# Products of zeros on TensorE ahead of the first transposes

## The chip, the cores and the metric

The kernel runs on one core of a Trainium2 chip. Its engines each work through their own list of instructions: TensorE (PE; its weight loads are shown as PEld), VectorE (DVE), ScalarE (ACT), GpSimd (POOL), and SyncE (SP), which here only issues transfers. They wait for each other by semaphores. The metric is the device time of one execution in microseconds, as the median of several.

## What is computed

One step of a streaming encoder layer for a prompt of 1024 tokens and a sample of 32, both 1024 wide. Cut to what stands at the start, which is where the change is:

```python
mod = silu(c) @ w_ada + b_ada                       # c: one row for the prompt, one for the sample
sh1, sc1, gt1, sh2, sc2, gt2 = split(mod, 6)        # six parts, each 1024 wide
h = rmsnorm(x, g_mix) * (1 + sc1) + sh1             # rmsnorm: x * rsqrt(mean(x * x) + EPS) * g
u = h @ w_in                                        # 1024 -> 5640 columns
# then band attention (8 heads), an mLSTM (4 heads), two gated branches, an output
# projection, a residual add, and the same pattern again with a SwiGLU feed-forward
```

All is float32. Large products are made from a high and a low part of each factor in a reduced float32 format (`F32R`), in three passes: high by high, low by high, high by low.

## The kernel before

**Tiling.** Prompt and sample form one matrix of 1056 columns (tokens), kept transposed: 8 blocks of 128 features on the partitions, tokens along the rows of memory. Products take the tokens in three tiles of 352 columns. [...]

**The start.** The order of work on TensorE, ScalarE, VectorE and GpSimd is the order in which the code writes it (a manual schedule); each engine runs its list strictly in that order. SyncE's transfers are issued in code order too.

- L222 to L229 issue the loads of the input, 8 blocks of 128 tokens (`xtok`, 512 KB each), and of the sample (`xsm`). Parameters go to `prow` from GpSimd's queue.
- `load_ada` (L276) issues 8 loads of `w_ada` of 1 MB each, one block of 128 rows each: the columns of the shift and the scale.
- The loop at L299 goes over four groups of two input blocks. For each it makes square sums on VectorE (`square_sum`, L288) and 16 transposes on TensorE (`x_transposes`, L296), four to one PSUM bank; ScalarE copies each bank to memory (L297). Three such banks (`mm`) are in turn.
- Between the third and the fourth group's transposes `param_cols` stands: TensorE transposes the parameters (L239), VectorE copies them (L240), ScalarE makes `csil`, the SiLU of `c` (L241). That copy stands between square sums 5 and 6 in VectorE's list.
- After the loop the sample is transposed (L310) and copied (L312), and GpSimd turns the square sums into the reciprocal roots `rstd` (L313, L314).
- `first_ada` (L331) walks over the 8 blocks of `w_ada`. In each step TensorE multiplies the scale's columns by `csil` (L337) into the PSUM tile `psA`, and VectorE adds the shift's columns times `csil` into two sums `acv` (L327 for the first block, L329 for the others). After the first step TensorE spreads `rstd` over the partitions (L257).
- `row_sums` (L363, L367), `first_shift` (L375) and `first_scale` (L380, L381) finish shift and scale. Then `first_units` (L482) makes the normed input block by block on VectorE and ScalarE (L390 to L409), and TensorE starts the products with `w_in` (L490). The weights' high and low parts for it come from `first_split` (L476) and `first_low` (L480) into tiles of the pool `wsp`, which has four buffers of 128x1024.
- SyncE also writes the transposed input to `xres` in device memory (L1540), once L312 is done.

**After the start.** All later products run through `unit` (L458) and similar loops (L906, L1843, L2089, L2246). Weight blocks are loaded ahead (L434) and split into parts on ScalarE (L424) and VectorE or GpSimd (L425).

Of the kernel before, what the change touches and what calls it, by code (L numbers as in the profile page):

```python
# [9 lines left out]
F32R = mybir.dt.float32r  # L10
BF16 = mybir.dt.bfloat16
# [6 lines left out]
P = 128  # L18
# [121 lines left out]
def hybrid_stream_step(  # L140
# [11 lines left out]
    pe, act, dve, pool, sp = nc.tensor, nc.scalar, nc.vector, nc.gpsimd, nc.sync  # L152
# [9 lines left out]
    wsp = ctx.enter_context(tc.tile_pool(name="wsp", bufs=4))  # L162
# [11 lines left out]
    def nm(s):  # L174
        uid[0] += 1
        return f"{s}_{uid[0]}"

    def slot(shape, dt=F32):
        return slots.tile(shape, dt, tag="s", name=nm("s"))

    def tmpt(shape=(P, T), dt=F32):
        return tmp.tile(list(shape), dt, tag="t", name=nm("t"))

    def mmt():
        return mm.tile([P, 512], F32, tag="mm", name=nm("mm"))
# [4 lines left out]
    def ps_t():  # L190
        return ps.tile([P, 1024], F32, tag="PT", name=nm("psT"))
# [4 lines left out]
    def f(ap):  # L196
        return ap.bitcast(F32)
# [12 lines left out]
    pool.memset(ssq, 1.0)  # L210


    prow = tmpt((P, P))
    xtok = []

# [60 lines left out]
    def load_ada(n):  # L276
        while len(was) < n:
            wa = slot([P, 2048])
            sp.dma_start(wa, w_ada[len(was) * P:(len(was) + 1) * P, 0:2048])
            was.append(wa)  # L280

    load_ada(KD)

    def square_sum(i):
        n = P if i < 8 else TS
        src = xtok[i] if i < 8 else xsm
        junk = tmpt((P, D), BF16)
        dve.tensor_tensor_reduce(junk[:n], src, src, 1.0, 0.0, ALU.mult, ALU.add, ssq[:n, i:i + 1])  # L288
# [18 lines left out]
    for j0 in range(0, KD, 4):  # L307
        pt = mmt()
# [142 lines left out]
    def unit(w, w0, xt, lo, hi, last=True):  # L451

        wt = W.use(w)
        pt = mmt()
        n = len(xt)
        for k in range(n):
            for q, (a, b) in enumerate(PASSES):
                pe.matmul(pt[:, :hi - lo], wt[(w0 + k) // 4][:, a, (w0 + k) % 4], xt[k][:, b, lo:hi],  # L458
                          start=(k == 0 and q == 0), stop=(k == n - 1 and q == 2))
            if k % 2 == 0 and k:  # L460
                side.flush(1)
            if k % 2 == 1:
                side.tick()
        if last:
            W.used(w)
        return pt[:, :hi - lo]
# [1308 lines left out]
    for pi, tiles in enumerate(parts):  # L1775
        if pi == 1:
            job = side.start(second_norm(parts[0]), 15, 50)
        for j in range(KD):
            for lo, hi in tiles:
                pt = unit(w_o[pi][j], 0, merged, lo, hi)  # L1780
# [50 lines left out]
    def bank(n=NT):  # L1831
        i = turn[0] % 8
        t = pb.tile([P, 512], F32, tag=f"b{i}", name=nm("psb")) if i < 5 else mmt()
        turn[0] += 1
        return t[:, :n]

    def times(w, x, acc, start=True, stop=True, onto=False):


        wt, = W.use(w)  # L1840
        for k in range(4):
            for q, (a, b) in enumerate(PASSES):
                pe.matmul(acc, wt[:, a, k], x[k][:, b], start=(start and not onto and k == 0 and q == 0),  # L1843
                          stop=(stop and k == 3 and q == 2), skip_group_check=onto)
        W.used(w)
        return acc
# [11 lines left out]
    def fifteen_products(x, rows, done, beside):  # L1858


        first = set()
        left = [(i, n) for ps in PARTS.values() for i, n, _ in ps]
        banks = {}
        for w, r in zip(x.blocks, x.FORMS):
            beside(r)
            if r in ONTO:
                y = times(w, FORMS[r], banks.pop(ONTO[r]), onto=True)
            else:
                y = times(w, FORMS[r], bank())
                banks[r] = y  # L1870
            complete = []
            for i, n, sign in PARTS[r]:
                c = rows[i][:, thirds[n]]
                if (i, n) not in first:
                    first.add((i, n))
                    if r == 8 and i == 1:
                        dve.tensor_copy(c, y)
                    else:
                        act.activation(c, y, AF.Copy, scale=float(sign))
                else:  # L1880
                    dve.tensor_tensor(c, c, y, op=ALU.add if sign > 0 else ALU.subtract)
                left.remove((i, n))
                if (i, n) not in left:
                    complete.append((i, n))
            run_put_off()
            put_off.extend(lambda z=z: done(*z) for z in complete)
# [34 lines left out]
    for i in range(0, len(fifteen), 2):  # L1921
# [5 lines left out]
        def run(x, rows):  # L1927
            fifteen_products(x, [y for _, _, y in rows], lambda i, n: rows[i][0].complete(*rows[i][1:], n), late_steps)
# [119 lines left out]
    for c in range(2):  # L2048
# [14 lines left out]
        x = times(a1, FORMS[14], bank())  # L2063
# [18 lines left out]
    for j in range(KD):  # L2082
        wt = W.use(w_d0[j])
        n = 0
        for i in range(2):
            acc = bank()
            for k in range(KP):
                for q, (u, v) in enumerate(PASSES):
                    pe.matmul(acc, wt[k // 4][:, u, k % 4], piece_of[k, i][:, v],  # L2089
                              start=(k == 0 and q == 0), stop=(k == KP - 1 and q == 2))  # L2090
# [144 lines left out]
    for j in range(KD):  # L2235
# [4 lines left out]
        for w, (k0, k1) in zip(w_d1[j], chunks):  # L2240
            wt = W.use(w)
            for k in range(k0, k1):
                while steps and (min(k + 4, NF - 1), 2) not in piece_of:
                    steps.pop(0)[2]()
                for q, (u, v) in enumerate(PASSES):
                    pe.matmul(acc, wt[(k - k0) // 4][:, u, (k - k0) % 4], piece_of[k, 2][:, v],  # L2246
                              start=(k == 0 and q == 0), stop=(k == NF - 1 and q == 2))
# [47 lines left out]
```

## Time and profile before

| what | value |
|---|---|
| time, median of 3 runs | 1606.86 us (1606.58 to 1607.44) |
| span of the profiled execution, first to last instruction | 1604.4 us |
| TensorE busy | 1576.2 us, 98% of the span |
| VectorE, ScalarE, GpSimd busy | 1135.5, 786.2, 445.3 us |
| TensorE's granted clock, mean | 0.999 |
| DMA, mean over the span | 120 GB/s |
| DMA, first two fortieths of the span | 362 and 273 GB/s |

The profile is of one execution. The median is 2.46 us longer than the profiled span; the time of the profiled execution itself is not recorded beside its span. "Busy" of TensorE is the union of the spans of its products, which overlap since they are pipelined, so that a row's mean duration (322 ns for a product of 352 columns) is longer than the distance from one product to the next.

A row of the timeline gives the start in microseconds from the span's start, the length, the engine, the line, the operation, what it writes and reads, the number of instructions merged into the row, and in brackets how long the engine was idle before it and what ended that.

### The profile page before, as it was taken

Reading aid. Unit: us, or ns where it says so; the run is one execution under the profiler, and the core shown is the slowest. Engines: PE = TensorE matmul, PEld = TensorE weight load, DVE = VectorE, ACT = ScalarE, POOL = GpSimd, SP = SyncE. Lnnn points to the kernel's source line nnn. Section 1 sums busy time; section 2 is a strip of 40 time slices with the busy share of each in tenths; the row PEclk is TensorE's granted clock in tenths of the full one; section 3 lists DMA queues with packets and bytes.
Section 4 is the critical chain, followed back from the end, with each engine's and each line's share of the span. In section 5 each row is a group of like instructions: output and inputs, shape, how many; then the busy total and the mean of one; then the engine's idle time right before and its main releaser. Section 6 shows DMA issues by size and latency. Waiting matters only on the chain.

```text
span 1604.4 us, 27406 instructions
## 1 busy us (share of the span) xinstructions
PE 1576.2 (98%) x10256; PEld 1554.8 (97%) x10256; DVE 1135.5 (71%) x2185; ACT 786.2 (49%) x1747; POOL 445.3 (28%) x477
## 2 busy tenths in 40 slices
PE   7999999999999999999999999999999999999997
PEld 6989999999999999999999999999999999999997
DVE  7766564646776855556654699988888986799754
ACT  3665463544455644444443655554544444545443
POOL 2344243433332411000012100566565650000001
PEclk9999999999999999999999999999999999999999
DMA  9823323232222232675353311313222227427453
GB/s 362 273 77 91 97 82 102 88 122 86 67 80 80 69 95 69 121 276 168 121 153 113 106 54 48 100 55 105 81 79 94 67 82 252 135 79 250 135 156 126
DMA packets 210414, 192.45 MB, mean 120 GB/s; under 512 B 10706, under 2 KB 180618, under 8 KB 209258
## 3 DMA queue, kind: packets, MB, share of 16 engines
q1 hardware_dynamic: 205386, 187.82, 37.4%
q10 hardware_dynamic: 4640, 2.82, 0.6%
q8 instruction: 81, 1.33, 0.4%
q14 instruction: 51, 0.42, 0.1%
q0 software_dynamic: 256, 0.06, 0.0%
HBM read 152.19 MB, written 41.63 MB: 121 GB/s over the span
## 4 chain that ended last, share of the span: by engine, by line
PE 88%; DVE 5%; DMA 3%; ACT 2%; issue 1%; SPq 0%; ACTq 0%; POOL 0%; DVEq 0%; POOLq 0%
PE mm L458 39%; PE psb L1843 18%; PE mm L1843 10%; PE mm L2246 3%; PE mm L906 3%; PE psb L2246 2%; PE psV L805 2%; PE psb L2089 2%; PE psS L747 1%; DMA s<-in_w_ada_dram 1%; PE psT L774 1%; PE mm L2089 1%; DMA wraw<-in_w_in_dram 1%; DMA t<-in_x_sample_dram 1%; DVE s L390 1%
## 5 line engine op out<-in xcount | busy, mean ns | idle before, releaser
L458 PE MATMUL mm<-s,wsp 128*128 128x352 f32 x4104 | 689.1, 324 | 0.0
L458 PEld LDWEIGHTS mm<-s,wsp 128*128 128x128 f32 x4104 | 656.9, 188 | 2.0 <-issue 0.4
L425 DVE TENSOR_TENSOR wsp<-wraw,wsp 128x512 fp32r<-128x512 f32 (+1 forms) x280 | 234.9, 855 | 120.0 <-ACT wsp L424 118.0
L1843 PE MATMUL psb<-s,wsp 128*128 128x352 f32 x1611 | 271.7, 322 | 1.5 <-DVE wsp L425 0.8
L424 ACT ACTIVATE wsp<-wraw 128x512 fp32r<-128x512 f32 x336 | 199.5, 617 | 141.5 <-PE psb L1843 44.0
L1843 PEld LDWEIGHTS psb<-s,wsp 128*128 128x128 f32 x1611 | 260.6, 188 | 2.1 <-DVE wsp L425 1.1
L1843 PE MATMUL mm<-s,wsp 128*128 128x352 f32 x933 | 159.3, 322 | 0.0
L1843 PEld LDWEIGHTS mm<-s,wsp 128*128 128x128 f32 x933 | 151.2, 188 | 0.5 <-DVE wsp L425 0.5
L767 POOL TENSOR_SCALAR st<-st,mx 128x640 f32<-128x640 f32 (+5 forms) x72 | 55.7, 774 | 184.8 <-DVE mx L766 170.5
L1229 DVE SCALAR_TENSOR_TENSOR t<-wa,cmix,t 128x512 f32<-128x512 f32 x112 | 89.1, 801 | 15.0 <-DMA wa<-in_w_ada_dram 14.6
L425 POOL TENSOR_TENSOR wsp<-wraw,wsp 128x512 fp32r<-128x512 f32 x56 | 75.8, 1374 | 49.4 <-ACT wsp L424 47.9
L762 ACT ACTIVATE st<-st,mx 128x640 f32<-128x640 f32 (+5 forms) x72 | 47.9, 666 | 71.6 <-DVE mx L761 70.3
L761 DVE CUSTOM_DVE_ANT_0 st<-psS,bias 128x640 f32<-128x640 f32 (+5 forms) x72 | 44.3, 616 | 46.1 <-PE psS L747 33.2
L1790 POOL TENSOR_TENSOR t<-t,sl 128x352 f32<-128x352 f32 x19 | 18.3, 961 | 185.3 <-DMA wraw<-in_w_out_dram 130.8
L781 ACT ACTIVATE pT<-psT 128x640 fp32r<-128x640 f32 (+3 forms) x80 | 38.6, 493 | 63.1 <-PE psT L774 47.7
L2158 POOL TENSOR_TENSOR fst<-fst 128x1 f32<-128x1 f32 (+1 forms) x6 | 1.2, 192 | 236.6 <-ACT t L2151 236.6
L786 DVE TENSOR_TENSOR pT<-psT,pT 128x640 fp32r<-128x640 f32 (+3 forms) x80 | 43.9, 557 | 22.5 <-ACT pT L781 22.3
L1452 POOL TENSOR_TENSOR wraw<-wraw,raw 128x512 f32<-128x512 f32 x33 | 55.8, 1702 | 0.9
L906 PE MATMUL mm<-s,s 128*128 128x264 f32 (+3 forms) x432 | 54.8, 283 | 0.0
L2246 PE MATMUL mm<-s,wsp 128*128 128x352 f32 x330 | 54.4, 324 | 0.0
L2246 PEld LDWEIGHTS mm<-s,wsp 128*128 128x128 f32 x330 | 53.1, 188 | 0.0
L1452 POOL TENSOR_TENSOR spare<-wraw 128x512 f32<-128x512 f32 x11 | 16.5, 1496 | 130.0 <-DMA wraw<-in_w_gate_up_dram 122.4
(396 smaller groups left out, 2561.3 us busy)
## 6 DMA issues: line engine op xcount, KB each, us to landing
wraw<-in_w_in_dram SPq DMA_DIRECT2D x38, 512.0 KB, 4.0
wraw<-in_w_gate_up_dram SPq DMA_DIRECT2D x33, 512.0 KB, 3.8
wa<-in_w_ada_dram SPq DMA_DIRECT2D x64, 256.0 KB, 2.9
wraw<-in_w_down_dram SPq DMA_DIRECT2D x32, 512.0 KB, 4.0
a_d<-t SPq DMA_DIRECT2D x22, 528.0 KB, 2.8
g_d<-t SPq DMA_DIRECT2D x16, 528.0 KB, 3.9
x<-xres SPq DMA_DIRECT2D x16, 528.0 KB, 6.7
t<-g_d SPq DMA_DIRECT2D x16, 528.0 KB, 5.4
```

The source lines that it names most:

```text
L424: act.activation(dst[:, 0], src, AF.Copy)
L425: eng.tensor_tensor(dst[:, 1], src, f(dst[:, 0]), op=ALU.subtract)
L458: pe.matmul(pt[:, :hi - lo], wt[(w0 + k) // 4][:, a, (w0 + k) % 4], xt[k][:, b, lo:hi], start=(k == 0 and q == 0), stop=(k == n - 1 and q ...
L761: dve.tensor_tensor_reduce(so, sv, bi, -1.0, 3.0e38, ALU.add, ALU.min, mx[:n, 1:2])
L762: act.activation(st[:n, :w], st[:n, :w], AF.Exp, bias=mx[:n, 1:2], scale=-1.0, accum_out=mx[:n, 2:3])
L767: pool.tensor_scalar(st[:n, :w], st[:n, :w], mx[:n, 3:4], 1.0, op0=ALU.mult, op1=ALU.mult)
L906: pe.matmul(pt[:n, :wd], hs[k][:, a, i * P:i * P + n], whl[b][:, k, :wd], start=(k == 0 and q == 0), stop=(k == KD - 1 and q == 2))
L1229: dve.scalar_tensor_tensor(ac[:, c], wa, cmix[:, c, k:k + 1], ac[:, c], op0=ALU.mult, op1=ALU.add)
L1452: self.eng.tensor_tensor(a(dst), a(x), a(y), op=op)
L1843: pe.matmul(acc, wt[:, a, k], x[k][:, b], start=(start and not onto and k == 0 and q == 0), stop=(stop and k == 3 and q == 2), skip_group_ ...
L2089: pe.matmul(acc, wt[k // 4][:, u, k % 4], piece_of[k, i][:, v], start=(k == 0 and q == 0), stop=(k == KP - 1 and q == 2))
L2246: pe.matmul(acc, wt[(k - k0) // 4][:, u, (k - k0) % 4], piece_of[k, 2][:, v], start=(k == 0 and q == 0), stop=(k == NF - 1 and q == 2))
```

## The change

A function `warm_up` is called after the loads of `w_ada` are issued and ahead of the loop over the four groups.

```diff
+    def warm_up():
+
+        z = wsp.tile([P, 1024], F32R, tag="wsp", name=nm("wsp"))
+        zb = z.bitcast(BF16)
+        dve.memset(f(z), 0.0)
+        pt = ps_t()
+
+        def run(x, w, n):
+            pe.matmul(pt[:, :n], w, x, start=True, stop=True)
+
+        for _ in range(12):
+            run(z[:, 0:352], z[:, 512:640], 352)
+        for o in (0, 8, 4, 16, 2):
+            for _ in range(5):
+                run(z[:, o:o + 352], z[:, 512:640], 352)
+        for o in (0, 8):
+            for _ in range(4):
+                run(z[:, o:o + 512], z[:, 520:648], 512)
+        for n in (352, 512):
+            for _ in range(5):
+                run(zb[:, 0:n], zb[:, 1024:1152], n)
...
     load_ada(KD)
+    warm_up()
```

VectorE fills one 128x1024 tile of the weight pool with zeros. TensorE then multiplies parts of that tile with each other: 37 products of 352 columns in `F32R`, 25 of them from shifted starts, 8 of 512 columns in `F32R`, and 5 each of 352 and 512 columns with the same bytes read as bfloat16. All write to one PSUM tile, which `first_ada` later takes for `psA`; nothing reads what they write. The lines behind the two places move down, by 22 and 23: L296 becomes L319, L239 becomes L261, L337 becomes L360.

TensorE's list from its beginning, before (`ident` is the identity, `s_92` and `s_95` hold input blocks, `mm` are PSUM banks):

```order
L2291 UNCONDITIONAL_BRANCH
L296 MATMUL mm_143<-ident,s_92 128x128 x4
L296 MATMUL mm_149<-ident,s_92 128x128 x4
L296 MATMUL mm_155<-ident,s_92 128x128 x4
L296 MATMUL mm_161<-ident,s_92 128x128 x4
L296 MATMUL mm_171<-ident,s_95 128x128 x4
```

The same list now, to the first transpose (`wsp_139` is the tile of zeros, `psT_141` the PSUM tile):

```order
L2314 UNCONDITIONAL_BRANCH
L221 MATMUL psT_141<-wsp_139 128x352 x37
L221 MATMUL psT_141<-wsp_139 128x512 x8
L221 LDWEIGHTS wsp_139
L221 MATMUL psT_141<-wsp_139 128x352
...
L221 LDWEIGHTS wsp_139
L221 MATMUL psT_141<-wsp_139 128x512
L319 MATMUL mm_201<-ident,s_92 128x128 x4
```

The 55 products stand ahead of all transposes; those of bfloat16 have a weight load of their own in the list. From the first transpose on the list is as before, with other line numbers.

VectorE's list from its beginning, before (ISA stands for the square sum and the reading of its result, `t` is scratch):

```order
L2291 UNCONDITIONAL_BRANCH
L288 ISA t_139,ssq<-s_92 128x1024
L288 ISA ssq 128x1
L288 ISA t_141,ssq<-s_92 128x1024
L288 ISA ssq 128x1
```

And now:

```order
L2314 UNCONDITIONAL_BRANCH
L217 MEMSET wsp_139 128x1024
L311 ISA t_197,ssq<-s_92 128x1024
L311 ISA ssq 128x1
L311 ISA t_199,ssq<-s_92 128x1024
```

One row came in front, and the rest is unmoved. The first product on TensorE waits for that memset. The lists of ScalarE, GpSimd and SyncE hold the same rows in the same order as before.

## The prediction

> **What bounds the kernel now.** I read the page first, for which engine sets the end.
>
> ```profile
> span 1604.4 us, 27406 instructions
> ...
> PE 1576.2 (98%) x10256; PEld 1554.8 (97%) x10256; DVE 1135.5 (71%) x2185; ACT 786.2 (49%) x1747; POOL 445.3 (28%) x477
> ...
> PE 88%; DVE 5%; DMA 3%; ACT 2%; issue 1%; SPq 0%; ACTq 0%; POOL 0%; DVEq 0%; POOLq 0%
> ```
>
> TensorE is busy for 98% of the span and carries 88% of the chain that ended last. The other 12% is what can bound a change at the start, so I next read the stretches before and after 50 us (second number of each row: TensorE's busy time).
>
> ```profile
> 0.00:50.00 50.00, 38.93 (x288) 1.00 0.93 345
> 50.00:1604.40 1554.40, 1537.30 (x9970) 1.00 0.37 113
> ```
>
> TensorE idles 11.1 us in the first 50 us and 17.1 us in all that follows, and in the first stretch the DMA engines are busy 93%. There the transfers set the pace. The timeline of the first 38 us, cut to the rows that the sum uses (start, length, engine, line; idle time before it in brackets):
>
> ```profile
> 0.81 1.28 ACT L297 ACT_TABLE_LOAD   x1 [0.81 <-PEq L2279]
> ...
> 4.58 0.45 PE L296 MATMUL mm<-ident,s 128*128 128x128 f32 x1 [4.58 <-DMA s<-in_x_prompt_dram]
> ...
> 5.77 7.46 PE L296 MATMUL mm<-ident,s 128*128 128x128 f32 x47 [0.74 <-DMA s<-in_x_prompt_dram]
> ...
> 9.24 4.75 ACT L297 ACTIVATE s<-mm 128x512 f32<-128x512 f32 x9 [0.22 <-PE mm L296]
> ...
> 13.06 0.27 PE L239 MATMUL psV<-ident,t 124*128 124x124 f32 x1
> ...
> 13.37 0.29 DVE L240 COPY cols<-psV 128x124 f32<-128x124 f32 x1 [0.71 <-PE psV L239]
> ...
> 14.61 2.10 PE L296 MATMUL mm<-ident,s 128*128 128x128 f32 x15 [1.16 <-DMA s<-in_x_prompt_dram]
> ...
> 15.30 0.22 ACT L241 ACTIVATE csil<-cols 128x16 f32<-128x16 f32 x1
> ...
> 15.42 2.04 ACT L297 ACTIVATE s<-mm 128x512 f32<-128x512 f32 x4
> ...
> 17.43 2.05 PE L337 MATMUL psT<-csil,s 128*128 128x128 f32 x16
> ...
> 17.51 1.42 DVE L327 TENSOR_SCALAR t<-s,csil 128x1024 f32<-128x1024 f32 x2 [0.43 <-ACT s L297]
> ...
> 19.97 2.48 DVE L329 SCALAR_TENSOR_TENSOR t<-s,csil,t 128x1024 f32<-128x1024 f32 x2 [1.04 <-DMA s<-in_w_ada_dram]
> ...
> 21.87 3.84 PE L337 MATMUL psT<-csil,s 128*128 128x128 f32 x32
> ...
> 23.62 14.14 DVE L329 SCALAR_TENSOR_TENSOR t<-s,csil,t 128x1024 f32<-128x1024 f32 x13 [1.16 <-DMA s<-in_w_ada_dram]
> ...
> 35.90 2.05 PE L337 MATMUL psT<-csil,s 128*128 128x128 f32 x16 [0.49 <-DMA s<-in_w_ada_dram]
> ```
>
> TensorE has nothing to do until 4.58 us, and then transposes the input as its rows land. From 17.4 to 38.0 us it and VectorE work through the eight blocks of `w_ada`, each pausing for a block's landing now and then. So a delay on TensorE before 17 us meets some slack in those pauses, and what exceeds it goes on, since after 38 us no transfer paces TensorE.
>
> **The change, part by part.** Of all engines only TensorE and VectorE get rows, and all of them stand ahead of the first transpose: one memset of 128x1024 on VectorE, then on TensorE 42 products 352 wide (12 + 25 + 5) and 13 that are 512 wide (8 + 5).
>
> *When they start.* The engines begin their own work at 0.81. The profile has no memset of that size on VectorE; the nearest rows (fourth field: busy, mean ns of one) bound it by 1.22 and 0.75 us:
>
> ```profile
> L288 DVE CUSTOM_DVE_ANT_0 t<-s 128x1024 bf16<-128x1024 f32 x8 | 9.6, 1224 | 5.3 <-DMA s<-in_x_prompt_dram 5.3
> ...
> L327 DVE TENSOR_SCALAR t<-s,csil 128x1024 f32<-128x1024 f32 x2 | 1.4, 750 | 0.4 <-ACT s L297 0.4
> ```
>
> I take 1.0, between them, and 0.1 for the signal: the products start at 1.9 us. [...] VectorE itself loses nothing: its first square sum waits for the input until 4.6 us.
>
> *What they take.* Products 352 wide follow each other closely in these pieces of the chain:
>
> ```profile
> 695.98 150.23 PE mm L458 x936
> ...
> 1004.40 9.59 PE psb L1843 x60
> ```
>
> 150.23/936 = 0.1605 us each, 0.456 ns a column. So 42 x 0.1605 = 6.7 us, and 13 x 0.1605 x 512/352 = 3.0 us: 9.8 us. No bfloat16 or oddly placed product is in the trace; I price them by column like the rest. They stand alone on TensorE, nothing hides them after 4.6 us.
>
> *The clock.* The granted clock is 1.00 in all stretches, but the transposes' durations are not one:
>
> ```profile
> L296 PE MATMUL mm<-ident,s 128*128 128x128 f32 x15 | 3.4, 419 | 0.7 <-DMA s<-in_x_prompt_dram 0.7
> L296 PE MATMUL mm<-ident,s 128*128 128x128 f32 x49 | 6.6, 282 | 1.3 <-DMA s<-in_x_prompt_dram 1.2
> ...
> 7.56 0.60 ACT L297 ACTIVATE s<-mm 128x512 f32<-128x512 f32 x1 [0.26 <-PE mm L296]
> 8.41 0.60 ACT L297 ACTIVATE s<-mm 128x512 f32<-128x512 f32 x1 [0.25 <-PE mm L296]
> ```
>
> The first row is of the stretch 5.7 to 9.0 us, the second of 9.1 to 17. Before 9.1 us four transposes take 8.41 - 7.56 = 0.85 us, 212 ns each; the products of L337 later follow each other at (2.05 - 0.27)/15 = 119 ns. TensorE thus starts 1.8 times slower, and gets its full pace 3.3 us after it became steadily busy (5.77), 4.5 us after its first product (4.58). The added products will pay this at their own start. For 4.5 us of it the loss is 4.5 x (1 - 119/212) = 2.0 us; for 3.3 us it is 1.4, for twice that 2.9. I take 2.0, since TensorE will be busy from its first product on. [...]
>
> So the transposes start at 1.9 + 9.8 + 2.0 = 13.7 us instead of 4.58. What they save by the full pace is 16 x 93 ns = 1.5 us in the first group, but that group was waiting for rows of the input anyhow, so it is worth nothing.
>
> *What the delay becomes.* By 13.7 us all of the input is there but its last block (its transposes had to wait for it until 14.61), so ScalarE's copies pace the transposes: (2.04 - 0.60)/3 = 0.48 us for four. The first copy starts at 13.7 + 0.65, the twelfth ends 11 x 0.48 + 0.60 later, at 20.2; L239 stood 0.93 us ahead of that end before (13.99 against 13.06), hence now at 19.3. That is 6.2 us late. From L239 on all is a chain that moves with it: VectorE's copy (its square sums 6 to 8 are queued behind that copy, and the reciprocal root behind them), `csil`, the last four copies, L310, L337 and L327. So L327 starts at 23.7 and L337 at 23.6.
>
> *What the pauses give back.* By then the blocks of `w_ada` land ahead of their use. VectorE loses its pauses of 1.04 and 1.16 us, 2.2 together. TensorE needs 7 x 16 x 119 ns = 13.3 us for the seven later blocks, where it took 37.95 - 21.87 = 16.1: it gets 2.7 back. The smaller one decides: 6.2 - 2.2 = 4.0 us late at 38 us, now bound by VectorE and TensorE and by no transfer.
>
> *What it costs later.* Two waits for transfers in the next stage can shrink, as these transfers were queued behind others and need not move:
>
> ```profile
> 70.76 1.15 ACT L424 ACTIVATE wsp<-wraw 128x512 fp32r<-128x512 f32 x2 [0.84 <-DMA wraw<-in_w_in_dram]
> ...
> 80.55 0.47 ACT L659 ACTIVATE t<-mm 128x352 f32<-128x352 f32 x1 [0.87 <-DMA wa<-in_w_ada_dram]
> ...
> 81.90 0.66 PE L700 MATMUL mm<-ident,t 128*128 128x128 f32 x4 [0.23 <-ACT s L662]
> ```
>
> Both are ScalarE's. TensorE's pause that hangs on them is 0.23 us, so I take 0.3 us off, with 0 and 0.9 as ends. The sum is 4.0 - 0.3 = 3.7 us.
>
> Edits at nothing: the zeroed tile takes one of four weight buffers, which the splits of L476 want at 36.8 us, 23 us after its last product; the PSUM tile is next written by TensorE itself. The writes of `xres` need L312, 6 us late at 24.4, and stood in SP's queue until 36.8.
>
> Ends of the sum: short memset (-0.25), 3.3 us of slow clock (-0.6), TensorE's 2.7 as slack (-0.5), 0.9 given back later (-0.6) make 1.8 us; long memset (+0.2), 6.6 us of slow clock (+0.9) and nothing given back (+0.3) make 5.1 us.
>
> **The rivals.** *The delay is swallowed downstream (not slower).* TensorE's 17.1 us of idle time after 50 us are where it would go; from 0.5 us more than I allow, the change is within 0.2%. For it speaks that the transfers of the next stage keep their time. Against it:
>
> ```profile
> PE psT L774 <- DVE pT L786: 1.3, 2, 1.0
> PE mm L1843 <- DVE x L1692: 1.1, 1, 1.1
> PE psT L774 <- POOL wsp L425: 0.9, 1, 0.9
> PE psV L805 <- DVE t L813: 0.8, 4, 0.2
> ```
>
> TensorE's longest waits after 50 us are for VectorE and GpSimd, whose work hangs on TensorE's own and moves with it; none is for a transfer. If two thirds or all went: 1606.9 to 1608.1 us.
>
> *Zeros do not raise the clock.* Then all 9.8 us run 1.8 times slower (17.5 us), the transposes start at 19.4 and pay the slow start themselves: of their 0.85 us for four, 0.37 exceeds the copies' pace, 1.5 us over four groups. 5.7 + 1.5 on top of 3.7 make 10.9: 1617.8 us. The profile holds no product of zeros, so nothing speaks for or against but that the transposes, mostly multiplications by zero, do raise it.
>
> *The later products run at another pace, because of what ran first.* 10,256 products: 0.3 ns on each is 0.2% of the time. The two pieces above differ by 0.7 ns (0.1605 and 0.1598); if all took the faster pace, 7.2 us would go, and with the delay 3.5 us remain as a gain: 1603.4 us, faster. Nothing in the trace shows a pace that outlives its cause.
>
> **How the numbers follow.** The profiled span is 1604.4 us, 2.5 less than the median of 1606.86; the delay lies within the span, so it is added to the median: 1606.86 + 3.7 = 1610.6 us. About 0.2% (3.2 us, up to 1610.1) can be told from no change. Chances: forecast 0.79, swallowed 0.12, zeros at the slow clock 0.05, another pace 0.04. The forecast's own ends are 1608.7 and 1612.0; about seven tenths of it lies above 1610.1, which with the slow clock makes 0.62 slower; the rest of it and the swallowed case make 0.34 the same; 0.04 faster. The range takes in the better part of the swallowed case and as much again above: 1607.8 to 1613.2.
>
> **What would show it.** In the new timeline: the memset from 0.81; the products from about 1.9 to 13.7 us, twofold slow for the first 3 to 7 us; L239's transpose at 19.3; no pause of VectorE for `w_ada`; its last piece and the first scale 4 us later than before; TensorE's products after 50 us at 0.160 us each, as many idle microseconds as before, less 0.3. The forecast is wrong if the products end by 10 us (the pauses would then swallow the delay), if the transposes still run at 212 ns, or if TensorE's idle time after 50 us shrinks by a microsecond or more.

## The result, and the profile after

The changed kernel takes 1627.15 us (median of 4 runs, 1626.58 to 1628.42), the kernel before, run beside it, 1607.12 us (1606.58 to 1607.44): a ratio of 1.0126, 95% interval 1.0114 to 1.0139. It is 20.0 us slower, where 3.7 were forecast. The profiled execution took 1627.24 us, with a span of 1625.2.

From its page: the span, the engines' busy time, the chain that ended last.

```profile
span 1625.2 us, 27517 instructions
...
PE 1587.7 (98%) x10311; PEld 1566.2 (96%) x10311; DVE 1139.5 (70%) x2186; ACT 784.5 (48%) x1747; POOL 459.7 (28%) x477
...
PE 89%; DVE 4%; ACT 2%; POOL 1%; issue 1%; DMA 0%; ACTq 0%; DVEq 0%; POOLq 0%
```

TensorE is busy 11.5 us longer than before (1587.7 against 1576.2) and idle 9.3 us longer (37.5 against 28.2); together that is the 20.8 us that the span grew. The 11.5 are about what the products of zeros take (11.89 us). The idle time was not forecast, and GpSimd (POOL) now has 1% of the chain, where it had 0%. The timeline of the first 60 us shows where:

```profile
1.10 0.91 DVE L217 MEMSET wsp<- 128x1024 f32 x1 [1.10 <-PEq L2302]
...
2.07 11.89 PE L221 MATMUL psT<-wsp 128*128 128x352 f32 x55 [2.07 <-DVE wsp L217]
...
13.79 5.86 PE L319 MATMUL mm<-ident,s 128*128 128x128 f32 x48
...
19.49 0.27 PE L261 MATMUL psV<-ident,t 124*128 124x124 f32 x1
...
22.01 0.40 POOL L265 COPY cmix<-csil 64x8 f32<-64x8 f32 x1 [15.94 <-ACT csil L263]
...
23.44 1.40 DVE L350 TENSOR_SCALAR t<-s,csil 128x1024 f32<-128x1024 f32 x2
...
23.95 3.49 PE L360 MATMUL psT<-csil,s 128*128 128x128 f32 x16
24.27 16.69 POOL L265 COPY cmix<-csil 64x8 f32<-64x8 f32 x1
24.76 16.14 DVE L352 SCALAR_TENSOR_TENSOR t<-s,csil,t 128x1024 f32<-128x1024 f32 x15
...
41.57 1.84 POOL L337 TENSOR_TENSOR rstd<-ssq,mhalf 128x9 f32<-128x9 f32 x1
43.46 2.21 PE L279 MATMUL mm<-ident,rstd 128*128 128x128 f32 x9 [16.02 <-POOL rstd L337]
...
45.60 13.66 PE L360 MATMUL psT<-csil,s 128*128 128x128 f32 x112
...
59.29 0.17 DVE L403 TENSOR_TENSOR s<-psT,cols 128x16 f32<-128x16 f32 x1 [18.39 <-PE psT L360]
```

To the start of the first 16 products of L360 all runs about as forecast. Then one small copy on GpSimd, 64 rows of 8 numbers, takes 16.69 us. It is the third of the four of `cmix` (L265, L266; L243, L244 before). It ends at 40.96, just when VectorE's run over `w_ada` does (24.76 + 16.14 = 40.90). Behind it in GpSimd's list stand the fourth copy and the two steps of the reciprocal roots (L336, L337); on the roots wait the nine products of L279, and behind these in TensorE's list the 112 products for the other seven blocks of `w_ada`. TensorE idles 16.02 us. The same place before (L257 is now L279, L380 is L403):

```profile
16.02 1.10 POOL L244 COPY cmix<-csil 64x8 f32<-64x8 f32 x1
...
17.17 0.18 POOL L243 COPY cmix<-csil 64x8 f32<-64x8 f32 x1
...
17.68 0.65 POOL L313 TENSOR_SCALAR ssq<-ssq 128x9 f32<-128x9 f32 x1
18.41 2.22 POOL L314 TENSOR_TENSOR rstd<-ssq,mhalf 128x9 f32<-128x9 f32 x1
...
20.69 1.26 PE L257 MATMUL mm<-ident,rstd 128*128 128x128 f32 x9 [1.21 <-POOL rstd L314]
...
37.99 0.17 DVE L380 TENSOR_TENSOR s<-psT,cols 128x16 f32<-128x16 f32 x1 [0.23 <-PE psT L337]
```

The third copy took 0.18 us there, and the roots were done at 20.63. The products with the roots moved from 20.69 to 43.46, by 22.8 us, and the first scale from 37.99 to 59.29, by 21.3. TensorE's longest wait between 17 and 62 us, from the answer on waits:

```profile
PE mm L279 <- POOL rstd L337: 16.0, 1, 16.0
```

And stretches of after (second number TensorE's busy time with its instructions, then weight loads, VectorE, ScalarE, GpSimd, the granted clock, the share of the DMA engines, GB/s), with the late stretch of before below:

```profile
24.00:28.00 4.00, 3.44 (x17) 3.25 (x16) 4.00 (x5) 0.61 (x7) 3.96 (x2) 0.62 1.02 424
28.00:44.00 16.00, 0.54 (x3) 0.54 (x4) 12.90 (x13) 0.00 (x0) 15.19 (x4) 0.58 0.91 312
64.00:1625.00 1561.00, 1543.93 (x10016) 1525.83 (x10015) 1106.77 (x2140) 768.73 (x1710) 433.03 (x454) 1.00 0.36 110
```

```profile
43.00:1604.00 1561.00, 1543.85 (x10015) 1525.53 (x10013) 1102.72 (x2140) 769.93 (x1710) 434.99 (x453) 1.00 0.37 114
```

In the middle stretch TensorE and ScalarE stand still while VectorE and GpSimd look busy; GpSimd's 15.19 us are the rest of the one copy, the fourth copy and the two steps of the roots. After the stage, TensorE does the same work in the same 1561 us.

### The profile page after: what moved, and what is told of

Same layout as the page of the kernel before. It is cut to its first block, busy times and chain, and to the rows that moved or that the text cites. A ratio compares the mean times of both kernels' runs of the same rounds, so it can differ in the third digit from the quotient of the medians.

```text
span 1625.2 us, 27517 instructions
## 1 busy us (share of the span) xinstructions
PE 1587.7 (98%) x10311; PEld 1566.2 (96%) x10311; DVE 1139.5 (70%) x2186; ACT 784.5 (48%) x1747; POOL 459.7 (28%) x477
## 4 chain that ended last, share of the span: by engine, by line
PE 89%; DVE 4%; ACT 2%; POOL 1%; issue 1%; DMA 0%; ACTq 0%; DVEq 0%; POOLq 0%
PE mm L481 40%; PE psb L1866 18%; PE mm L1866 10%; PE mm L2269 3%; PE mm L929 3%; PE psb L2269 2%; PE psV L828 2%; PE psb L2112 2%; PE psS L770 1%; PE psT L797 1%; PE mm L2112 1%; POOL cmix L265 1%; PE psT L360 1%; DVE st L784 1%; PE psV L1163 1%
## 5 line engine op out<-in xcount | busy, mean ns | idle before, releaser
L1475 POOL TENSOR_TENSOR wraw<-wraw 128x512 f32<-128x512 f32 x22 | 32.6, 1482 | 72.3 <-DVE wsp L448 71.4
```

The lines of the kernel that those rows point to most:

```text
L1475: self.eng.tensor_tensor(a(dst), a(x), a(y), op=op)
```

## Experiments

Theory A: GpSimd's small operations need openings in VectorE's work. Before the change VectorE's pauses for landing blocks of `w_ada` gave them; with the delay all blocks are there, the pauses go, and what GpSimd has not done when the run begins waits for its end. The rivals stand in the expectations. The kernel before took 1606.61, 1606.72 and 1606.44 us in the three sets of runs. L numbers are each kernel's own.

**VectorE waits for the roots.** If A holds, adding a wait to the changed kernel makes it faster.

```diff
     def first_ada():
         first_load()
+        seen = cp.tile([P, 1], F32, name="seen")
+        dve.tensor_copy(seen, rstd[:, 0:1])
         for k in range(KD):
```

> The changed kernel with one VectorE copy of a column of the reciprocal roots ahead of the first product of w_ada, so that VectorE stands still until GpSimd has made the roots. Theory A (GpSimd's small operations are kept out while VectorE runs its two-input operations back to back): the third copy into cmix takes under 0.5 us instead of 16.7, TensorE's spreading of the roots starts near 27 us instead of 43.5, VectorE ends its share of w_ada near 44.5 us; in all 6 us over the kernel before, 1613 us (1612 to 1615), that is some 14 us faster than the changed kernel although a wait was added. Theory B (the zeros or the long product run ahead of the transposes slow what follows, by clock or otherwise): a wait more on VectorE cannot help, 1627 us or more. Theory C (the copy is slow because transfers fill the memory at that time): the copy stays long, and VectorE now waits for it: over 1640 us.

Measured: 1613.06 us, ratio 1.004 (1.0026 to 1.0054). Its timeline:

```profile
24.00 1.84 POOL L337 TENSOR_TENSOR rstd<-ssq,mhalf 128x9 f32<-128x9 f32 x1
25.87 0.15 DVE L357 COPY seen<-rstd 128x1 f32<-128x1 f32 x1 [2.77 <-POOL rstd L337]
25.89 1.25 PE L279 MATMUL mm<-ident,rstd 128*128 128x128 f32 x9 [0.42 <-POOL rstd L337]
```

VectorE stands for 2.77 us, and in that pause GpSimd does all its work; TensorE's wait falls from 16.02 to 0.42 us. With 2.77 us of waiting added, the kernel is 14 us faster than the changed one: the stall is most of the loss. Theories B (1627 us or more) and C (over 1640) fall.

**The roots first.** The roots are taken out of the crowded place: all nine square sums and both root steps are written ahead of the transposes.

```diff
+    for i in range(9):
+        square_sum(i)
+    pool.tensor_scalar(ssq, ssq, 1.0 / D, EPS, op0=ALU.mult, op1=ALU.add)
+    pool.tensor_tensor(rstd, ssq, mhalf[:, :NB], op=ALU.pow)
     for g in range(4):
-        for i in range(2):
-            square_sum(2 * g + i)
...
-    square_sum(8)
...
-    pool.tensor_scalar(ssq, ssq, 1.0 / D, EPS, op0=ALU.mult, op1=ALU.add)
-    pool.tensor_tensor(rstd, ssq, mhalf[:, :NB], op=ALU.pow)
```

> The changed kernel with all nine square sums and the reciprocal roots written ahead of the transposes and of the copies into cmix, so that GpSimd makes the roots near 17 to 20 us, before VectorE's run over w_ada. The 55 products of zeros stay. Theory A: the roots are there when TensorE wants them; only the delay of the prediction is left, plus 3 to 4 us over the kernel before: 1610.5 us (1609.5 to 1612). One of the copies into cmix still takes some 16 us, and nobody waits for it. Theory B (zeros or products as such): 1625 us or more, as the products are unchanged. Theory C (transfers): the roots, made while transfers are as dense, take many microseconds, over 1615 us.

Measured: 1608.12 us (11 runs, 1607.65 to 1610.4), ratio 1.0015 (1.0006 to 1.0023).

```profile
17.61 1.84 POOL L325 TENSOR_TENSOR rstd<-ssq,mhalf 128x9 f32<-128x9 f32 x1
...
22.00 1.42 DVE L349 TENSOR_SCALAR t<-s,csil 128x1024 f32<-128x1024 f32 x2 [1.89 <-ACT csil L263]
...
22.85 0.62 POOL L265 COPY cmix<-csil 64x8 f32<-64x8 f32 x1
...
23.51 1.16 POOL L266 COPY cmix<-csil 64x8 f32<-64x8 f32 x1
```

The roots are done by 19.45, and all but 1.5 us of the 20 go. That is less than the 3 to 4 us expected to stay: VectorE's square sums are out of the way too, and it begins with `w_ada` at 22.00 instead of 23.44. But no copy of `cmix` was caught this time, though the fourth began while VectorE's run was on; it took 1.16 us. That part of the expectation missed: an unbroken run alone does not shut GpSimd out.

**The delay without the products.** The kernel before, with one transpose of a late input block written ahead of all others; no zeros, no widths, no types.

```diff
+    pt = ps_t()
+    pe.transpose(pt[:, :P], xtok[6][:, :P], ident)
     for g in range(4):
```

> The kernel before, without any product of zeros; instead one transpose that waits for the seventh input block stands first, so that TensorE's transposes start near 13.5 us as in the changed kernel, and at the slow clock. Theory A: what costs is when the transposes start, so the parameters' transpose comes near 20.5 us, GpSimd's copy is kept out again for some 16 us and the time is that of the changed kernel, 1627 us (1624 to 1630). Theory B (zeros, widths, addresses or types of the products): only the late start is left, 1611 us (1609 to 1613).

Measured: 1628.74 us, ratio 1.0138 (1.0124 to 1.0151).

```profile
25.33 16.69 POOL L243 COPY cmix<-csil 64x8 f32<-64x8 f32 x1
25.82 16.14 DVE L331 SCALAR_TENSOR_TENSOR t<-s,csil,t 128x1024 f32<-128x1024 f32 x15
...
44.53 2.21 PE L257 MATMUL mm<-ident,rstd 128*128 128x128 f32 x9 [17.60 <-POOL rstd L316]
```

The same copy is caught for the same 16.69 us. The loss hangs on how late the transposes start, and on nothing that was multiplied.

**A probe in the kernel before.** One more small copy on GpSimd when block 4 of `w_ada` is used.

```diff
             if k == 0:
                 bcast_cols(RB, rstd, [P] * 8 + [TS], 0)
+            if k == 4:
+                probe = cp.tile([P, 8], F32, name="probe")
+                pool.tensor_copy(probe[:DH], was[4][:DH, 0:8])
```

> The kernel before, with one more small GpSimd copy (64x8) of the fifth block of w_ada into a tile of its own, which nothing reads; it can start when that block lands, near 28.4 us, while VectorE is in its run over w_ada and until that run ends near 37.8 us GpSimd has no other work. Theory A: the copy takes until VectorE's run ends, 8 to 9.5 us, where such a copy took 0.2 to 0.4 us; the time stays within 0.1% of the kernel before, since nothing waits for it. Theory B and C' (a GpSimd copy waits at most for one VectorE operation): 0.2 to 1.5 us.

Measured: 1606.78 us, ratio 1.0 (0.9991 to 1.0009). The probe ran in 0.18 us. It started at 28.17, with the landing that VectorE waits for too, and so perhaps in a short pause: VectorE's row of ten operations there, 12.27 us from 23.39 on, is some 0.2 to 0.3 us longer than ten at 1.19 us from start to start. It tells little.

**The copies on ScalarE.** If only those copies can be caught, this frees the roots.

```diff
         for c in range(2):
-            pool.tensor_copy(cmix[:DH, c], csil[:DH, :, c])
-            pool.tensor_copy(cmix[DH:, c], csil[DH:, :, 1 - c])
+            act.activation(cmix[:DH, c], csil[:DH, :, c], AF.Copy)
+            act.activation(cmix[DH:, c], csil[DH:, :, 1 - c], AF.Copy)
```

> The changed kernel with the four copies into cmix moved from GpSimd to ScalarE, where they stand behind csil and push the last input copies back by about 0.8 us; GpSimd keeps the two steps of the reciprocal roots. They can start at 23.5 us, when VectorE begins with w_ada. Theory A (VectorE's run keeps GpSimd out as a whole): the roots are stuck to the run's end near 41 us, 1626 us (1624 to 1629). Theory A' (a GpSimd operation waits only for the VectorE operation that is under way, and the 16.7 us were something of that one copy): the roots are there by 28 us, 1612 us (1610 to 1614).

Measured: 1626.85 us, ratio 1.0125 (1.0111 to 1.0139).

```profile
24.39 18.29 POOL L337 TENSOR_TENSOR rstd<-ssq,mhalf 128x9 f32<-128x9 f32 x1
...
42.74 2.21 PE L279 MATMUL mm<-ident,rstd 128*128 128x128 f32 x9 [13.43 <-POOL rstd L337]
```

Now the root itself is caught, 18.29 us instead of 1.84. It is not that copy, but whatever GpSimd has in hand there.

**One of VectorE's two sums in PSUM.** VectorE accumulates two sums of 128x1024 in turn; the first goes to PSUM, so that every second operation reads one tensor of SBUF, not two. The row sums read the other sum for both, so the shift that they make is not the reference's.

```diff
-    acv = [tmpt((P, D)) for _ in range(2)]
+    acv = [ps_s(), tmpt((P, D))]
...
-            pe.matmul(sum_at[b // 4][:, at:at + DH], acv[c][:, b * P:(b + 1) * P],
+            pe.matmul(sum_at[b // 4][:, at:at + DH], acv[1][:, b * P:(b + 1) * P],
```

> The changed kernel with one of VectorE's two running sums over w_ada in PSUM, so that every other operation of the run reads only one operand from SBUF (the other reads two, as before); the row sums read the other sum in its place, so that the shift is wrong. [...] Theory A'' (any unbroken run of VectorE keeps GpSimd out): the copy takes 15 us or more, 1627 us.

Measured: 1610.14 us (10 runs, 1609.17 to 1610.99), ratio 1.0021 (1.0012 to 1.003).

```profile
25.02 2.17 POOL L337 TENSOR_TENSOR rstd<-ssq,mhalf 128x9 f32<-128x9 f32 x1
25.40 1.26 DVE L352 SCALAR_TENSOR_TENSOR psS<-s,csil,psS 128x1024 f32<-128x1024 f32 x1
26.59 1.27 DVE L352 SCALAR_TENSOR_TENSOR t<-s,csil,t 128x1024 f32<-128x1024 f32 x1
```

VectorE's run is as unbroken as in the changed kernel, at 1.19 us from start to start, yet the root takes 2.17 us and nothing is caught. So VectorE's being busy is not enough to keep GpSimd off. That what VectorE reads and writes in SBUF decides it fits this run but is not shown by it: VectorE's first operation, now into PSUM, takes 1.27 us instead of 0.74, and GpSimd's operations meet the run at other points (the third copy starts at 23.70, in the changed kernel at 24.27). The time is below the 1611 to 1617 us that the author expected for GpSimd coming through at every other operation, since the copies were hardly held (0.70 us for the third, 0.19 us for the fourth).

**Probes inside the run.** The roots first, as above, and eight times, inside VectorE's run, two steps on ScalarE and a GpSimd copy that waits for them.

```diff
                 bcast_cols(RB, rstd, [P] * 8 + [TS], 0)
+                pc = ps_s()
+                for i in range(8):
+                    src, dst = (cp.tile([P, 8], F32, name=f"probe{n}{i}") for n in "ab")
+                    act.activation(pc[:, :512], was[0][:, :512], AF.Copy)
+                    act.activation(src, pc[:, :8], AF.Copy)
+                    pool.tensor_copy(dst[:DH], src[:DH])
```

> The kernel with the roots made early, and in VectorE's run over w_ada, from about 29.5 us on, eight small GpSimd copies (64x8), each started by a ScalarE operation, about 0.85 us apart, so that they come at different phases of VectorE's operations (1.2 us each, back to back until 39.5 us, with no transfer to wait for). Nothing reads them. Theory A: the first is stuck to the run's end, some 10 us, and the others follow it within 0.3 us each. Theory A': each takes 0.2 to 1.3 us, by the phase at which it starts. The time stays that of the kernel without them, 1608 us (1607 to 1610.5).

Measured: 1609.57 us (10 runs, 1607.11 to 1610.46), ratio 1.0014 (1.0005 to 1.0023). The timeline, then the answer on the probes' line (shortest, median and longest, in ns):

```profile
24.08 16.15 DVE L351 SCALAR_TENSOR_TENSOR t<-s,csil,t 128x1024 f32<-128x1024 f32 x15
...
30.62 8.33 POOL L375 COPY probeb<-probea 64x8 f32<-64x8 f32 x8 [5.22 <-ACT probea L374]
```

```profile
L375 POOL COPY probeb<-probea x8: 453/1252/1254, 30.6 to 38.5; 64x8 f32<-64x8 f32 x8
```

Each probe gets through, at the price of about one VectorE operation, and VectorE loses nothing (16.15 us against 16.14). A in its strict form falls: what arrives within the run is held for one operation. What was caught elsewhere began 0.83 to 1.44 us after VectorE's first operation on `w_ada`; but so did the third copy with the roots first (22.85, after 22.00), and that took 0.62 us.

**The first 12 products alone.**

```diff
         for _ in range(12):
             run(z[:, 0:352], z[:, 512:640], 352)
-        for o in (0, 8, 4, 16, 2):
...
-                run(zb[:, 0:n], zb[:, 1024:1152], n)
```

> The changed kernel with only the first 12 products of zeros (352 wide, all from one place), and without the other widths, starts and types. They run at half pace from 2.06 to about 5.6 us, before the second input block lands. Theory A (the damage comes from the late start of what follows): the transposes are not delayed, the first group runs at full pace but waits for its rows as before, and the time is that of the kernel before, 1606.6 us (1605.5 to 1607.5). Theory B (products of zeros as such cost): a good part of the 20 us stays.

Measured: 1607.27 us (11 runs), ratio 1.0005 (0.9996 to 1.0014). The products run from 2.06 to 5.54, and the first scale stands at 37.96: the input's landing hides them.

**The first 27 products.**

```diff
-        for o in (0, 8, 4, 16, 2):
+        for o in (0, 8, 4):
             for _ in range(5):
                 run(z[:, o:o + 352], z[:, 512:640], 352)
-        for o in (0, 8):
...
```

> The changed kernel with 27 of its products of zeros (352 wide in F32R), which should end near 8.5 us instead of 13.7. The parameters' transpose then comes near 14.3 us instead of 19.5, 1.2 us later than in the kernel before, and VectorE still has to wait for the second and third block of w_ada for about 1 us in all. Theory A: in these pauses GpSimd finishes, nothing is stuck, and the delay is swallowed by the pauses: 1607 us (1606 to 1608.5). A cost in proportion to the products (theory B): 27 of 55 products would cost some 10 us, 1617 us.

Measured: 1607.38 us (10 runs, 1606.52 to 1611.73), ratio 1.0011 (1.0002 to 1.002).

```profile
20.09 2.94 POOL L331 TENSOR_TENSOR rstd<-ssq,mhalf 128x9 f32<-128x9 f32 x1
...
23.44 14.31 DVE L346 SCALAR_TENSOR_TENSOR t<-s,csil,t 128x1024 f32<-128x1024 f32 x13 [0.93 <-DMA s<-in_w_ada_dram]
```

About half the products, and under a tenth of the loss: the cost does not grow in proportion. VectorE still pauses 0.93 us for a block, and the root, 2.94 us long, is done before that pause ends.

**What lets a caught operation go.** In the changed kernel VectorE clears a PSUM tile when it comes to block 4: 0.48 us in which its operation has no operand in SBUF, without waiting for anything.

```diff
+            if k == 4:
+                dve.memset(ps_s()[:, :512], 0.0)
             if k < KD - 1:
```

> The changed kernel with one VectorE memset of a PSUM tile (128x512, some 0.6 us, no operand in SBUF) in the middle of the run over w_ada, ahead of the fifth block, near 32 us; nothing reads it. VectorE gets no wait and no pause, and 0.6 us more work. [...] Theory E (only a true pause of VectorE lets it in): the copy ends with the run again and the memset is added, 1628 us.

Measured: 1627.45 us, ratio 1.0131 (1.0116 to 1.0147).

```profile
24.45 17.19 POOL L265 COPY cmix<-csil 64x8 f32<-64x8 f32 x1
24.94 7.25 DVE L352 SCALAR_TENSOR_TENSOR t<-s,csil,t 128x1024 f32<-128x1024 f32 x6
32.29 0.48 DVE L363 MEMSET psS<- 128x512 f32 x1
32.70 8.89 DVE L352 SCALAR_TENSOR_TENSOR t<-s,csil,t 128x1024 f32<-128x1024 f32 x9
```

Neither the memset nor the 0.10 us ahead of it, in which the rows show VectorE idle (24.94 + 7.25 = 32.19), let the copy in, though elsewhere this copy takes 0.18 us. Once caught, it waits for the end of the run, at 41.59.

**Is it the change of operation?** The copy was caught where VectorE goes from L350's form, with one SBUF tensor, to L352's, with two. Here the first block takes the two-tensor form as well, adding the zeroed tile.

```diff
         if k == 0:
-            dve.tensor_scalar(o, w, x, None, op0=ALU.mult)
+            dve.scalar_tensor_tensor(o, w, x, f(zeros), op0=ALU.mult, op1=ALU.add)
```

> The changed kernel with the first block of w_ada multiplied by VectorE's operation with two tensor inputs, adding the tile of zeros, in place of the form with one tensor and a scalar; the run then holds one form of operation alone, from 23.4 us on, and gets some 1.1 us longer. Theory F (the copy was caught at the change of form, from the operation with one tensor input, 0.75 us for 1024 elements, to the one with two): GpSimd now gets one operation in at each of VectorE's, 1.2 us apart, the roots come by 30 us, 1614 us (1611 to 1617). Theory A (an unbroken run that GpSimd meets from its start keeps it out whatever the form): stuck to 42 us, 1628 us.

Measured: 1628.75 us, ratio 1.0138 (1.0121 to 1.0155).

```profile
24.23 1.16 POOL L266 COPY cmix<-csil 64x8 f32<-64x8 f32 x1
25.43 17.16 POOL L267 COPY cmix<-csil 64x8 f32<-64x8 f32 x1
```

The third copy now takes 1.16 us, and the fourth is caught. It is not the change of form.

**Another order of the same operations.** The first sum's blocks 0 and 1 come first, then the second sum's, so that in these four each second operation depends on the one in front of it.

```diff
-            if k < KD - 1:
+            if k == 0:
+                shift_part(0, 0, 0, KD)
+            elif k == 1:
+                shift_part(1, 0, 0, KD)
+                shift_part(0, 1, 0, KD)
+                shift_part(1, 1, 0, KD)
+            elif k < KD - 1:
```

> The changed kernel with VectorE's four operations on the first two blocks in another order: the form with one tensor input, the one with two, then again one and two. The work is the same. Theory F (caught at the change from one input to two): there are two such changes now, and a GpSimd copy that waits at one of them is stuck to the run's end or to the next operation with one input: 1627 us if it is the second that catches it, down to 1613 us if the copies come through at the operation with one input. Theory A: stuck as before, 1627 us (1625 to 1629).

Measured: 1613.33 us, ratio 1.0043 (1.0028 to 1.0058).

```profile
24.17 1.28 DVE L352 SCALAR_TENSOR_TENSOR t<-s,csil,t 128x1024 f32<-128x1024 f32 x1
...
25.37 0.75 DVE L350 TENSOR_SCALAR t<-s,csil 128x1024 f32<-128x1024 f32 x1
25.60 0.58 POOL L336 TENSOR_SCALAR ssq<-ssq 128x9 f32<-128x9 f32 x1
26.15 14.96 DVE L352 SCALAR_TENSOR_TENSOR t<-s,csil,t 128x1024 f32<-128x1024 f32 x14
26.27 2.88 POOL L337 TENSOR_TENSOR rstd<-ssq,mhalf 128x9 f32<-128x9 f32 x1
```

The same work in another order, with gaps of 0.03 us where one operation waits for the one before it (25.37 + 0.75 = 26.12, next at 26.15), is 13.8 us faster than the changed kernel: the root takes 2.88 us, and is not caught. Theory A, by which 1627 us were expected, falls here too.

## Why the prediction was wrong

**Right: the start.** The memset took 0.91 us (1.0 taken), the products started at 2.07 (1.9), 0.06 us behind it (0.1), the transposes at 13.79 (13.7), L261 stood at 19.49 (19.3), L350 at 23.44 (23.7), L360 at 23.95 (23.6). The term for the slow start nearly holds too; the answers on the products' line, for its first 3.5 us and for the rest, give

```profile
L221 PE MATMUL psT<-wsp x12: 495/495/663, 2.1 to 5.5; 128*128 128x352 f32 x12
...
L221 PE MATMUL psT<-wsp x43: 312/324/495, 5.8 to 13.6; 128*128 128x352 f32 x25, 128*128 128x512 f32 x8, 128*128 128x352 bf16 x5, 128*128 128x512 bf16 x5
```

and 11.89 us in all, against 9.8 + 2.0. The slow pace lasted from 2.07 to about 5.8 us, 3.7 us where 4.5 were taken. That it could last 6.6 us, as in the long end of the sum, was the author's estimate, and no run shows it. Nor is it shown that a clock sets this pace: from 2.07 to 5.80 us the granted clock reads 1.00. With zeros alone the products' duration fell from 495 to 324 ns, so the rival "Zeros do not raise the clock" falls: the pace rose without other work.

**Right: VectorE's pauses go.** Its last piece of `w_ada` ends at 40.90, where before it ended at 37.76 (23.62 + 14.14). That is 3.1 us late; 4.0 were forecast.

**Failed: "From L239 on all is a chain that moves with it".** In this chain, "the reciprocal root behind them" was taken to move with L239 at its old length, and so to end near 26.8 (20.63 + 6.2). It ended at 43.41. The sum then had VectorE's two pauses as pure gain, and TensorE's seven later blocks as free to run. But in TensorE's list the products with the roots stand between the first block and the other seven, and nothing in the sum priced GpSimd's four copies and two root steps once VectorE runs without a pause. The pauses were counted as slack of VectorE; they were also the time in which GpSimd's root ran (18.41 to 20.63, with VectorE's pause of 1.04 us ending at 19.97). With the stall gone, the time comes out near the sum, in part by luck. One sum in PSUM, with the products and the delay unchanged, moves the first scale from 37.99 to 41.44 by its trace, 3.45 us, and takes 1610.14 us where 1610.6 were forecast; but VectorE's first operation is 0.5 us longer there, which the sum does not have, and without it VectorE would be about 2.9 us late, where 4.0 were forecast.

**Right: what comes later.** From the first scale (21.3 us later) to the span (20.8 us longer) 0.5 us are given back; 0.3 were forecast. Nothing downstream swallowed a delay even of this size, and the later products kept their pace (1543.93 us busy against 1543.85): both these rivals fall. No rival had an operation of GpSimd in it. The row for it was there: the second copy at 1.10 us against 0.18 for the third, in the kernel before.

**What stays open.** That the delayed start lets VectorE run without a pause, that GpSimd then loses its place, and that the roots behind it hold TensorE, is shown: by the run in which VectorE waits, by the one with the roots first, and by the delay without products. That it is over access to SBUF is the author's estimate from the sum in PSUM, one kernel in which the root took 2.17 us, and is not shown. Why one GpSimd operation near the run's beginning is held for all of it, and another there or later for one or two operations, is not settled. It isn't the kind of GpSimd operation (a copy was held for 16.69 us, the root for 18.29) or the change of VectorE's form (17.16 us without one), and an operation of VectorE outside SBUF, 0.48 us long, did not end it. No version tried beats the kernel before.

The rows hold one more sign, which no run tested as a cause. In the five kernels with a held operation VectorE shows no pause from its copy of the parameters (19.80 us in the changed kernel) to the moment when the operation was caught. With the roots first VectorE had stood for 1.89 us just ahead of `w_ada`; there the third copy began 0.17 us into VectorE's second operation on `w_ada` (22.85 after 22.00 + 1.42 - 0.74 = 22.68), just as in the changed kernel (24.27 after 24.10), and took 0.62 us instead of 16.69. In the other order of operations two gaps of 0.03 and 0.04 us came just ahead of the fourth copy and of the root, which got through. So a pause ahead may keep an operation from being caught, where one of 0.10 us behind did not free it. The sum in PSUM is the exception: there VectorE shows no pause, and nothing was held.

## What to carry to other kernels

A pause of one engine may be another's opening: before you count a pause as slack to be used up, look for short operations of GpSimd around it whose durations vary (here 0.18 to 1.10 us for copies of one size), and for who waits behind them. When a change closes the pauses ahead of a long unbroken run on VectorE, do the GpSimd work that others wait for before the run, or leave one pause: 2.77 us of waiting bought 14 us here. Moving only a part of it (the copies to ScalarE) left the rest to be caught. A delay's cost need not grow in proportion: here 12 products cost nothing that could be told from no change, 27 cost 1 us by the medians, 55 cost 20.

## What the runs showed of the hardware

- GpSimd operations that took 0.18 to 1.84 us elsewhere took 16.69 to 18.29 us beside VectorE operations of at most 1.27 us each that followed each other closely (five kernels: the changed one and four of the experiments), while VectorE itself was not slowed (16.14 us for the 15, against 16.15 in the run in which VectorE waits and nothing is held). In other kernels of this case an operation that came within such a run waited for about one of them: a copy took 1.16 us with the roots first, the probes 1.25 us at the median.
- A memset of 128x1024 float32 on VectorE took 0.91 us, 0.89 ns for each of the 1024 columns.
- The granted clock fell to 0.62 between 24 and 28 us in the changed kernel, after a stretch in which TensorE's longest wait was 1.36 us. The first 16 products of L360 took 3.49 us there, against 2.05 before. It is not so in each run: with the same wait of 1.36 us, these products took 2.05 us in the run in which VectorE waits and in the delay without products. The profiled run with the roots first, at 1609.53 us, shows the fall too (0.62, and 3.51 us), and so pays some 1.5 us that the forecast did not have.
